# A transformer layer on one core: GpSimd's elementwise work on VectorE, quotients of the mixer's outputs on one engine, their sums of squares a block later, and one PSUM bank per head for these outputs

## The chip, the cores and the metric

One core of a Trainium2 chip. The time is microseconds of device time of one execution, as a median over runs. An engine (TensorE = PE, VectorE = DVE, ScalarE = ACT, GpSimd = POOL) takes its instructions in a fixed order; SyncE's queue (SP) issues all transfers between HBM and SBUF.

## What is computed

One layer of a hybrid backbone, for 128 context tokens and 2,048 latent tokens of width 1,024, in float32. Cut to what matters:

```python
shift1, scale1, gate1, shift2, scale2, gate2 = split(mod, 6)     # mod = silu(c) @ w_mod + b_mod
h = rmsnorm(x, norm1) * (1 + scale1) + shift1
z = h @ w_in                       # sc_b, sc_c, sc_x, q, k, v, o, gates
y_sc = sc_b * conv3(sc_c * sc_x)   # short convolution
# mLSTM, both directions, 4 heads of 128, chunks of 128 tokens:
s = (q @ k.T) * exp(dlog - m_t)
num = s @ v + w_inter * (C @ q);  den = s.sum(-1) + w_inter * (n @ q)
h_m = num / max(abs(den), exp(-m_t))
h_m = rmsnorm_per_head(h_fwd + h_bwd) * mh_norm * sigmoid(o)
x = x + gate1 * (concat(y_sc, h_m) @ w_out)
h2 = rmsnorm(x, norm2) * (1 + scale2) + shift2
a, g = split(conv3(h2 @ w_up), 2)                                # d_ff = 2816
x = x + gate2 * ((silu(g) * a) @ w_down)
y = rmsnorm(x, final_norm)
```

## The kernel before

Every large product is made of three products with operands that carry fewer bits: a float32 `a` is split into a high part `aH` (a ScalarE copy into the type that TensorE takes) and a low part `aL = a − aH` (a subtraction), and TensorE adds up `wh·hH + wh·hL + wl·hH`. So each tile of weights and of tokens costs a copy on ScalarE and a subtraction on VectorE or GpSimd before its matmuls can start. `gemm` (L192 to L199) is one block of such a product: 24 matmuls of up to 384 columns into one PSUM bank `acc`, out of a pool of four.

The program is recorded stage by stage and a scheduler then sets the order on each engine; buffers in rotation (a pool's `bufs`) decide when an instruction may start. The stages in the order of time: modulation, values and gates (vg), k, q and short convolution of the second half of the tokens (0 to some 355 us); vg of the first half; the gates' scans; **Sums** (34 units, L697 and L708: gated sums of keys and values, chunk by chunk and for a pair of heads); **Mix** (34 units, the outputs, 690 to 1020 us); the rest of the output projection and the sums of tokens for the up-projection (L229 to L236); the up-projection (L938 to L940, 44 units `j` of seven half-size products each, Strassen's scheme; weights' parts at L276, token splits at L258, drains of the banks `pa`, `pb`, `pc` at L943, L948 and L950); the down-projection (L1030 to L1032, weights' parts at L991 and L993).

Sums and Mix are short chains over several engines, so `weave` (L810) runs them as a software pipeline and puts blocks out of a list between them: q and o of the first half, its short convolution, and out_proj of four of the six token groups, 92 blocks in all, one per step in Sums, four per three steps in Mix.

A Mix unit is written in four parts, which `weave` gives to successive steps:

- load: q, k, v, the row tile `R` (512 KB, broadcast from HBM), the states.
- first: TensorE makes the scores `S` (L753); GpSimd adds the mask to the first half of `R` (L754); ScalarE takes four exponentials (L758); VectorE scales q by the second half of `R` into `qs` (L761) and multiplies the scores by the exponentials (L762).
- second: TensorE makes the outputs `y` of both heads and directions with the row sums in a 129th column (L773, L775), in a tile of two banks of which there is one; VectorE updates the state `sf` (L779), takes the divisors `den` (L783 to L785); then per head ScalarE multiplies the first direction by its reciprocal (L790), VectorE adds the second (L791), ScalarE takes the sum of squares (L793); L794 on VectorE scales it and adds EPS, GpSimd takes the power −1/2 (L795), ScalarE applies it (L797).
- third: TensorE transposes (L803), VectorE applies mh_norm and the gate o (L805), and the result is stored.

In out_proj, VectorE adds a block onto the residual (L433), ScalarE squares it (L440), and VectorE adds the squares up (L441) right behind; the statistics then sum over partitions by matmuls with ones (L122), of which those of the last group (`late`) stand ahead of the up-projection's first unit (they are called at `i == 4` of the products' loop, ahead of that product).

GpSimd's elementwise work, all of it subtractions or additions of two SBUF tiles: L108 (low parts of weights), L181 (low parts of tokens), L235 (one of the sums of tokens), L276 for three of the seven parts, L754, L993 for 704 of 1,408 columns. PSUM has eight banks: four `acc`, one `st`, one `S`, two for `y`; the jobs of mod_dve at the start (L499) write their unused product into `y` too.

## Time and profile before

| what | value |
|---|---|
| median of 3 runs | 2623.24 us (2619.05 to 2626.44) |
| the profiled execution: its span | 2622.1 us |
| TensorE busy | 2539.1 us |
| VectorE, ScalarE, GpSimd busy | 1501.3, 1066.1, 706.4 us |
| moved between HBM and SBUF | 403.25 MB, 154 GB/s |

The profiled execution is one run of its own: its time is the span, 2622.1 us from the first to the last instruction, and 1.1 us below the median. Busy time is the time in which an engine worked on an instruction; TensorE's ends are modelled. A row of waits names the waiting engine, tile and line, then what ended the wait, then the total, the number of times and the longest. A row of groups has count, busy time, mean length in ns, and the idle time ahead with its causes. The granted clock is a share of TensorE's full speed.

### The profile page before, as it was taken

Reading aid. Unit: us, or ns where it says so; the run is one execution under the profiler, and the core shown is the slowest. Engines: PE = TensorE matmul, PEld = TensorE weight load, DVE = VectorE, ACT = ScalarE, POOL = GpSimd, SP = SyncE. Lnnn points to the kernel's source line nnn. Section 1 sums busy time; section 2 is a strip of 40 time slices with the busy share of each in tenths; the row PEclk is TensorE's granted clock in tenths of the full one; section 3 lists DMA queues with packets and bytes.
Section 4 is the critical chain, followed back from the end, with each engine's and each line's share of the span. In section 5 each row is a group of like instructions: output and inputs, shape, how many; then the busy total and the mean of one; then the engine's idle time right before and its main releaser. Section 6 shows DMA issues by size and latency. Waiting matters only on the chain. (4 is left out here: it accounts for less than half of the span.)

```text
span 2622.1 us, 46918 instructions
## 1 busy us (share of the span) xinstructions
PE 2539.1 (97%) x18511; PEld 2519.2 (96%) x18511; DVE 1501.3 (57%) x2560; ACT 1066.1 (41%) x2028; POOL 706.4 (27%) x534
## 2 busy tenths in 40 slices
PE   8999999999988988899999999999999999999998
PEld 7999999999988988899999999999999999999998
DVE  3993242333457666797686669666666635353533
ACT  4521142322345454464454446554544523232411
POOL 2542242211333344221121112111111222232232
PEclk9999999999999999999999999999999999999999
DMA  8773142555467887854252224222222635454442
GB/s 280 250 254 101 57 140 85 155 180 155 152 195 242 253 256 235 267 195 139 84 178 91 79 79 165 83 83 82 83 83 90 234 113 184 156 179 150 149 139 77
DMA packets 223582, 403.25 MB, mean 154 GB/s; under 512 B 20722, under 2 KB 144770, under 8 KB 221698
## 3 DMA queue, kind: packets, MB, share of 16 engines
q1 hardware_dynamic: 223362, 400.25, 46.5%
q8 instruction: 145, 2.38, 0.4%
q14 instruction: 75, 0.61, 0.1%
HBM read 305.13 MB, written 95.04 MB: 153 GB/s over the span
## 5 line engine op out<-in xcount | busy, mean ns | idle before, releaser
L196 PE MATMUL acc<-hH,wh 128*128 128x384 f32 (+1 forms) x1536 | 516.4, 336 | 0.0
L198 PE MATMUL acc<-hH,wl 128*128 128x384 f32 (+1 forms) x1536 | 505.0, 329 | 0.0
L197 PE MATMUL acc<-hL,wh 128*128 128x384 f32 (+1 forms) x1536 | 504.7, 329 | 0.0
L938 PE MATMUL pa<-tH,wh 128*128 128x272 f32 x1408 | 410.1, 291 | 5.6 <-DVE raw L950 5.2
L940 PE MATMUL pa<-tH,wl 128*128 128x272 f32 x1408 | 409.3, 291 | 0.4 <-DVE wl L276 0.4
L1030 PE MATMUL d<-uh,wh 128*128 128x272 f32 x1408 | 406.0, 288 | 3.1 <-ACT raw L948 3.1
L939 PE MATMUL pa<-tL,wh 128*128 128x272 f32 x1408 | 407.1, 289 | 0.0
L1032 PE MATMUL d<-uh,wl 128*128 128x272 f32 x1408 | 406.9, 289 | 0.0
L1031 PE MATMUL d<-ul,wh 128*128 128x272 f32 x1408 | 404.4, 287 | 0.0
L276 POOL TENSOR_TENSOR wl<-st,wh 128x512 fp32r<-128x512 f32 x132 | 182.3, 1381 | 730.5 <-ACT wh L275 697.5
L108 POOL TENSOR_TENSOR wl<-wst,wh 128x512 fp32r<-128x512 f32 (+1 forms) x160 | 234.3, 1486 | 434.0 <-ACT wh L105 421.5
L196 PEld LDWEIGHTS acc<-hH,wh 128*128 128x128 f32 x1536 | 291.1, 190 | 1.5 <-issue 0.4
L197 PEld LDWEIGHTS acc<-hL,wh 128*128 128x128 f32 x1536 | 291.1, 189 | 1.0
L198 PEld LDWEIGHTS acc<-hH,wl 128*128 128x128 f32 x1536 | 290.5, 189 | 0.2 <-issue 0.2
L938 PEld LDWEIGHTS pa<-tH,wh 128*128 128x128 f32 x1408 | 266.8, 190 | 6.4 <-issue 5.7
L1030 PEld LDWEIGHTS d<-uh,wh 128*128 128x128 f32 x1408 | 266.9, 190 | 3.4 <-ACT raw L948 3.3
L939 PEld LDWEIGHTS pa<-tL,wh 128*128 128x128 f32 x1408 | 267.3, 190 | 0.0
L940 PEld LDWEIGHTS pa<-tH,wl 128*128 128x128 f32 x1408 | 266.6, 189 | 0.6 <-DVE wl L276 0.6
L1032 PEld LDWEIGHTS d<-uh,wl 128*128 128x128 f32 x1408 | 266.1, 189 | 0.1
L1031 PEld LDWEIGHTS d<-ul,wh 128*128 128x128 f32 x1408 | 265.3, 188 | 0.0
L993 POOL TENSOR_TENSOR wl<-st,wh 128x704 fp32r<-128x704 f32 x64 | 150.5, 2352 | 367.2 <-ACT wh L991 358.2
L884 DVE SCALAR_TENSOR_TENSOR tt<-raw,fw,tt 128x127 f32<-128x127 f32 (+4 forms) x264 | 245.7, 959 | 1.5 <-ACT tt L890 0.8
(215 smaller groups left out, 5031.6 us busy)
## 6 DMA issues: line engine op xcount, KB each, us to landing
st<-in_w_up SPq DMA_DIRECT2D x88, 512.0 KB, 4.4
st<-in_w_down SPq DMA_DIRECT2D x64, 704.0 KB, 4.2
wst<-in_w_in SPq DMA_DIRECT2D x48, 512.0 KB, 4.1
us<-uD SPq DMA_DIRECT2D x88, 272.0 KB, 4.4
R<-nD SPq DMA_DIRECT2D x34, 512.0 KB, 5.5
wm<-in_w_modr SPq DMA_DIRECT2D x32, 512.0 KB, 4.7
F<-tD SPq DMA_DIRECT2D x12, 1088.0 KB, 8.8
uD<-tt SPq DMA_DIRECT2D x22, 576.0 KB, 2.8
```

Of the source, the lines that this page charges most:

```text
L108: G.tensor_sub(wl[:, a:a + n // 2], st[:, a:a + n // 2], wh[:, a:a + n // 2].bitcast(F32))
L196: PE.matmul(acc[:, :n], w_h, hH[:, k, :n], start=(k == 0), stop=False)
L197: PE.matmul(acc[:, :n], w_h, hL[:, k, :n], start=False, stop=False)
L198: PE.matmul(acc[:, :n], w_l, hH[:, k, :n], start=False, stop=(k == KT - 1))
L276: (G if on_pool else V).tensor_sub(wl, a, wh.bitcast(F32))
L884: V.scalar_tensor_tensor(o, i, w, o, op0=ALU.mult, op1=ALU.add)
L938: PE.matmul(acc, wh[:, w], rh, start=(kk == 0 and i in (0, 1, 5)), stop=False, skip_group_check=True)
L939: PE.matmul(acc, wh[:, w], rl, start=False, stop=False, skip_group_check=True)
L940: PE.matmul(acc, wl[:, w], rh, start=False, stop=(kk == 3), skip_group_check=True)
L1030: PE.matmul(acc[b][:, :NB], wh[:, c], uh[:, q], start=(j == 0), stop=False)
L1031: PE.matmul(acc[b][:, :NB], wh[:, c], ul[:, q], start=False, stop=False)
L1032: PE.matmul(acc[b][:, :NB], wl[:, c], uh[:, q], start=False, stop=(j == FT - 1))
```

## The change

- All of GpSimd's subtractions and additions of tiles (L108, L181, L235, L276, L754, L993) go to VectorE, 434 instructions. GpSimd keeps the powers, and takes the addition of EPS (L811 after) that VectorE had (L794).
- ScalarE's step of the quotient (L790) becomes a VectorE step (L800 after); the divisors are taken per head, and stand, with the quotients, in the program ahead of the update of `sf` (L806 after). The division by 128 moves into the scale of the square.
- Each head's `y` has a bank of its own, out of three in rotation, and the Sums' products too, with two ScalarE copies for one. `acc` has three banks in rotation instead of four; in the start stage there is a pool `pj` besides, with a fourth `acc` and the two banks that mod_dve writes.
- out_proj hands its sum of squares to a list `pend`, which is emptied after the next block's output.
- The late statistics are called after the second product and may not be issued before its last matmul.
- `weave` takes a pattern: (1, 0, 1) blocks in three steps of Sums, (2, 1, 2) in Mix.

```diff
@@ weights
-            G.tensor_sub(wl[:, a:a + n // 2], st[:, a:a + n // 2], wh[:, a:a + n // 2].bitcast(F32))
+            V.tensor_sub(wl[:, a:a + n // 2], st[:, a:a + n // 2], wh[:, a:a + n // 2].bitcast(F32))
...
-            (G if on_pool else V).tensor_sub(wl, a, wh.bitcast(F32))
+            V.tensor_sub(wl, a, wh.bitcast(F32))
...
-                for e, a, b in ((G, 0, 704), (V, 704, n)):
-                    e.tensor_sub(wl[:, a:b], st[:, a:b], wh[:, a:b].bitcast(F32))
+                for a, b in ((0, 704), (704, n)):
+                    V.tensor_sub(wl[:, a:b], st[:, a:b], wh[:, a:b].bitcast(F32))
@@ accumulators
+    def accumulator():
+        pool = pa[next(turn_a) % len(pa)]
+        return pool.tile([P, 512], F32, name="acc")
...
-        pa = ph1.enter_context(tc.tile_pool(name="pa", bufs=4, space=PSUM))
+        pa = [ph1.enter_context(tc.tile_pool(name=f"pa{i}", bufs=1, space=PSUM)) for i in range(3)]
+        turn_a = count()
...
+        py = phr.enter_context(tc.tile_pool(name="py", bufs=3, space=PSUM))
@@ out_proj
                         Q.dma_start(xD[m][:, t0:t0 + n], xr[:, :n])
+                        while pend:
+                            pend.pop()()
...
-                            V.tensor_add(ss[:, :n], ss[:, :n], sq[:, :n])
+                            pend.append(lambda ss=ss[:, :n], sq=sq[:, :n]: V.tensor_add(ss, ss, sq))
@@ Mix
-                G.tensor_add(W, W, bc(maskN[:, None], [P, 2, 2, P]))
+                V.tensor_add(W, W, bc(maskN[:, None], [P, 2, 2, P]))
...
-                y = pm.tile([P, 2, 512], F32, name="y")
+                ys = [py.tile([P, 512], F32, name="y") for _ in range(2)]
...
+                for h, y in enumerate(ys):
+                    yv = y[:, :258].rearrange("p (d n) -> p d n", d=2)
+                    den = mb.tile([P, 2], F32, name="den", bufs=4)
+                    V.tensor_tensor(den, yv[:, :, 128], em[:, h], op=ALU.max)
+                    V.scalar_tensor_tensor(den, yv[:, :, 128], -1.0, den, op0=ALU.mult, op1=ALU.max)
+                    V.reciprocal(den, den)
+                    V.tensor_scalar(hv[:, h], yv[:, 0, :P], den[:, 0:1], None, op0=ALU.mult)
+                    V.scalar_tensor_tensor(hv[:, h], yv[:, 1, :P], den[:, 1:2], hv[:, h],
+                                           op0=ALU.mult, op1=ALU.add)
                 if 0 <= c < NL - 1:
...
-                    S.activation(hv[:, h], yv[:, h, 0, :P], AF.Copy, scale=den[:, h, 0:1])
...
-                V.tensor_scalar(ss, ss, 1.0 / P, EPS, op0=ALU.mult, op1=ALU.add)
+                    S.activation(sj, hv[:, h], AF.Square, scale=P ** -0.5, accum_out=ss[:, h:h + 1])
+                G.tensor_scalar(ss, ss, EPS, None, op0=ALU.add)
@@ weave
-                next(fill, None)
-                if extra and i % extra == 0:
+                for _ in range(blocks[i % 3]):
                     next(fill, None)
...
-        weave([Sums(c, hp) for c in range(NL - 1, -2, -1) for hp in range(2)], fill, 0)
-        weave([Mix(c, hp) for c in range(-1, NL) for hp in range(2)], fill, 3)
+        weave([Sums(c, hp) for c in range(NL - 1, -2, -1) for hp in range(2)], fill, (1, 0, 1))
+        weave([Mix(c, hp) for c in range(-1, NL) for hp in range(2)], fill, (2, 1, 2))
@@ products
-            if late and i == 4:
-                late.pop()()
...
+            if late and i == 1:
+                with tc.issue_after(mm.ins):
+                    late.pop()()
```

Where the instructions stand, first on TensorE, at a unit in the middle of Mix. Before (names: `S` scores, `st` the transposes of an earlier unit, `y` outputs, `acc` a projection block; in brackets the semaphores that an instruction waits for, one or more per engine or transfer queue):

```order
L198 MATMUL acc<-hH,wl 128x384
L753 MATMUL S<-q_8408,k_8404 128x128 [waits DMAHW4_49,DMAHW1_49,DVE_49]
L753 MATMUL S<-q_8408,k_8404 128x128
L803 MATMUL st<-ident,hv 128x128 [waits DVE_49,Activation_49]
L803 MATMUL st<-ident,hv 128x128 [waits Activation_49]
L773 MATMUL y<-sf_4848,qs 128x129 [waits DVE_49,PE_49]
L775 MATMUL y<-v_8321,R 128x129 [waits DMAHW2_49,DMAHW0_49]
L773 MATMUL y<-sb,qs 128x129 [waits DMAHW6_49]
L775 MATMUL y<-v_8321,R 128x129
L773 MATMUL y<-sf_4848,qs 128x129
L775 MATMUL y<-v_8321,R 128x129
```

After, at such a place (L768 is L753 of before, L820 is L803, L791 is L773, L793 is L775):

```order
L202 MATMUL acc<-hH,wl 128x384
L768 MATMUL S<-q_7995,k_7991 128x128 [waits DMAHW7_49,DMAHW1_49,DVE_49]
L768 MATMUL S<-q_7995,k_7991 128x128
L820 MATMUL st<-ident,hv 128x128 [waits DVE_49,Activation_49]
L820 MATMUL st<-ident,hv 128x128 [waits Activation_49]
L791 MATMUL y<-sf_4857,qs 128x129
L793 MATMUL y<-v_7903,R 128x129 [waits DMAHW5_49,DMAHW3_49]
L791 MATMUL y<-sb,qs 128x129 [waits DMAHW6_49]
L793 MATMUL y<-v_7903,R 128x129
L791 MATMUL y<-sf_4857,qs 128x129 [waits DVE_49,PE_49]
L793 MATMUL y<-v_7903,R 128x129
```

The first `y` matmul of a unit no longer waits on VectorE; the wait stands at the first matmul of the second head.

VectorE at such a unit, before (L433 a projection block's output, L762 the scores, L805 the output of an earlier unit, L441 a sum of squares, L779 the state, L783 to L785 the divisors, L791 the quotient):

```order
L762 TENSOR_TENSOR R<-S,R 128x2x256 [waits PE_49,Pool_49]
L805 SCALAR_TENSOR_TENSOR o_9103<-st,mhn,o_9103 128x128 [waits DMAHW3_49,PE_49]
L441 TENSOR_TENSOR ss<-ss,sq 128x384 [waits Activation_49]
L805 SCALAR_TENSOR_TENSOR o_9103<-st,mhn,o_9103 128x128
L779 SCALAR_TENSOR_TENSOR sf_4848<-sf_4848,decB,sb 128x129 [waits DMAHW2_49,PE_49]
L779 SCALAR_TENSOR_TENSOR sf_4848<-sf_4848,decB,sb 128x129 [waits PE_49]
L783 TENSOR_TENSOR den<-y,cols 128x4 [waits PE_49]
L761 TENSOR_TENSOR qs<-R,q_9346 128x512 [waits DMAHW3_49,DMAHW2_49]
L784 SCALAR_TENSOR_TENSOR den<-y,den 128x4 [waits DVE_49]
L785 RECIPROCAL den<-den 128x4 [waits DVE_49]
L791 SCALAR_TENSOR_TENSOR hv<-y,den,hv 128x128 [waits Activation_49] x2
```

After (L438 is L433 of before, L777 is L762, L822 is L805, L797 to L799 are the divisors, L806 is L779, L800 and L801 are the quotient):

```order
L438 SCALAR_TENSOR_TENSOR row<-acc,modT,row 128x384 [waits DMAHW6_49,DMAHW3_49,PE_49]
L777 TENSOR_TENSOR R<-S,R 128x2x256 [waits PE_49]
L822 SCALAR_TENSOR_TENSOR o_9575<-st,mhn,o_9575 128x128 [waits DMAHW1_49,PE_49]
L822 SCALAR_TENSOR_TENSOR o_9575<-st,mhn,o_9575 128x128
L797 TENSOR_TENSOR den<-y,cols 128x2 [waits PE_49]
L806 SCALAR_TENSOR_TENSOR sf_4857<-sf_4857,decB,sb 128x129
L798 SCALAR_TENSOR_TENSOR den<-y,den 128x2 [waits DVE_49]
L797 TENSOR_TENSOR den<-y,cols 128x2 [waits PE_49]
L799 RECIPROCAL den<-den 128x2 [waits DVE_49]
L806 SCALAR_TENSOR_TENSOR sf_4857<-sf_4857,decB,sb 128x129
L800 TENSOR_SCALAR hv<-y,den 128x128 [waits DVE_49]
L798 SCALAR_TENSOR_TENSOR den<-y,den 128x2
```

The divisors are taken head by head, the quotients wait for VectorE alone, and no sum of squares stands ahead of them.

A little later on VectorE, after (L108 a weight's low part, L769 the mask add that was L754 on GpSimd, L776 is L761 of before):

```order
L108 TENSOR_TENSOR wl<-wst,wh 128x512 [waits DMAHW0_49]
L108 TENSOR_TENSOR wl<-wst,wh 128x512
L438 SCALAR_TENSOR_TENSOR row<-acc,modT,row 128x384 [waits DMAHW7_49,PE_49]
L769 TENSOR_TENSOR R<-R,maskN 128x2x256 [waits DMAHW0_49]
L776 TENSOR_TENSOR qs<-R,q_9832 128x512 [waits DMAHW5_49]
L108 TENSOR_TENSOR wl<-wst,wh 128x512 [waits DMAHW2_49]
L438 SCALAR_TENSOR_TENSOR row<-acc,modT,row 128x384 [waits DMAHW3_49,DMAHW1_49,PE_49]
L777 TENSOR_TENSOR R<-S,R 128x2x256 [waits DVE_49,PE_49,Activation_49]
```

The mask add waits for a transfer in VectorE's order, directly ahead of the step that reads the same tile, and ahead of drains.

TensorE from the last projection block to the up-projection, before (L122 late statistics, L938 to L940 the first product):

```order
L198 MATMUL acc<-hH,wl 128x256
L122 MATMUL st<-ones,ss 128x1 [waits DVE_49,PE_49]
L122 MATMUL st<-ones,ss 128x1 x2
L938 MATMUL pa<-tH,wh 128x272 [waits DMAHW4_49,DMAHW3_49,DMAHW5_49,DMAHW1_49,DMAHW6_49,DMAHW0_49,DMAHW7_49,DVE_49,Activation_49]
L939 MATMUL pa<-tL,wh 128x272
L940 MATMUL pa<-tH,wl 128x272 [waits Pool_49]
```

After (L952 to L954 are L938 to L940):

```order
L954 MATMUL pb<-tH,wl 128x272
L122 MATMUL st<-ones,ss 128x1 x3
L952 MATMUL pa<-tH,wh 128x272 [waits DMAHW4_49,DMAHW3_49,DMAHW5_49,DMAHW2_49,DMAHW7_49,DMAHW0_49,Activation_49]
L953 MATMUL pa<-tL,wh 128x272 [waits DVE_49]
L954 MATMUL pa<-tH,wl 128x272
L122 MATMUL st<-ones,ss 128x1 [waits DVE_49]
```

The late statistics now stand behind the 48 matmuls of the first two products, and three more of the third product stand between their parts.

More of the change, by code (lines that the diff above doesn't have):

```diff
@@ L189, in make_h @@
         return apply(b, load_x(b, src, xp, "xt", 2), norm)
+    def accumulator():
+        pool = pa[next(turn_a) % len(pa)]
+        return pool.tile([P, 512], F32, name="acc")
     def gemm(w, h, n):
         (wh, wl), (hH, hL) = w, h
-        acc = pa.tile([P, 512], F32, name="acc")
+        acc = accumulator()
         for k in range(KT):
@@ L328, in vg @@
                         o = c * P - BL[b][0]
-                        acc = pa.tile([P, 512], F32, name="acc")
+                        acc = accumulator()
                         for k in range(KT):
@@ L449, in hymba_kernel @@
         hs = {}
-        with tc.tile_pool(name="start", bufs=1, side="right") as stp:
+        with tc.tile_pool(name="start", bufs=1, side="right") as stp, \
+                tc.tile_pool(name="pj", bufs=1, space=PSUM) as pj:
+            pa.append(pj)
             def mod_pe(mt):
@@ L453, in mod_pe @@
                 Q.dma_start(st, I["w_mod"][mt])
-                ps = pa.tile([P, 512], F32, name="acc")
+                ps = accumulator()
                 for k in range(KT):
@@ L705, in second @@
                 c, hp = self.c, self.hp
-                pk = pm.tile([P, 2, 512], F32, name="y")
+                pk = [py.tile([P, 512], F32, name="y") for _ in range(2)]
                 for h in range(2):
-                    PE.matmul(pk[:, h, :258], self.kT[:, h * P:(h + 1) * P],
+                    PE.matmul(pk[h][:, :258], self.kT[:, h * P:(h + 1) * P],
                               self.vw[:, h].rearrange("p d n -> p (d n)"), start=True, stop=True)
@@ L767, in second @@
                 self.o2 = load2(mb, "o2", oD, c + 1, hp)
-                y = pm.tile([P, 2, 512], F32, name="y")
-                for h in range(2):
+                ys = [py.tile([P, 512], F32, name="y") for _ in range(2)]
+                em = colsel(self.cols, EM, max(c, 0), hp)
+                hv = self.hv = mb.tile([P, 2, P], F32, name="hv", bufs=3)
+                ss = mb.tile([P, 2], F32, name="hss", bufs=2)
+                for h, y in enumerate(ys):
                     for d in range(2):
-                        o = y[:, h, d * 129:(d + 1) * 129]
+                        o = y[:, d * 129:(d + 1) * 129]
                         if c >= 0:
@@ L939, in hymba_kernel @@
                     PE.matmul(acc, wh[:, w], rl, start=False, stop=False, skip_group_check=True)
-                    PE.matmul(acc, wl[:, w], rh, start=False, stop=(kk == 3), skip_group_check=True)
+                    mm = PE.matmul(acc, wl[:, w], rh, start=False, stop=(kk == 3), skip_group_check=True)
                 if i < 3:
```

62 lines of the change are left out of this document (29 added, 33 removed).

## The prediction

> **What bounds the kernel now.** First the page: the span, then the busy time of the engines (busy us, share of the span, instructions).
>
> ```profile
> span 2622.1 us, 46918 instructions
> PE 2539.1 (97%) x18511; PEld 2519.2 (96%) x18511; DVE 1501.3 (57%) x2560; ACT 1066.1 (41%) x2028; POOL 706.4 (27%) x534
> ```
>
> TensorE is busy for 97%, and the change takes no matmul away. All that can be won is what TensorE waits (2622.1 − 2539.1 = 83 us) and what it loses to a lower granted clock. So I read its list of waits next (total us, times, longest).
>
> ```profile
> PE y L773 <- DVE hv L791: 33.3, 14, 6.9
> PE st L122 <- DVE ss L441: 8.3, 3, 6.5
> PE pa L938 <- DVE raw L950: 5.2, 3, 1.9
> PE acc L335 <- POOL hL L181: 2.2, 1, 2.2
> PE S L697 <- ACT kT L699: 0.6, 1, 0.6
> ```
>
> One row stands out: the first matmul of a mixer unit's output (L773) waits 33.3 us for the step on VectorE that empties the previous unit's `y` (L791). Where, and at what clock, the windows tell: stretch and length, busy time of PE, PEld, DVE, ACT, POOL with their counts, granted clock, DMA share, GB/s.
>
> ```profile
> 66.00:197.00 131.00, 130.47 (x888) 129.88 (x887) 124.73 (x209) 46.48 (x93) 61.70 (x47) 1.00 0.77 251
> 690.00:1020.00 330.00, 296.30 (x1890) 292.68 (x1889) 204.16 (x526) 166.26 (x499) 127.25 (x111) 0.96 0.73 229
> 850.00:858.00 8.00, 5.99 (x33) 5.78 (x32) 4.54 (x15) 3.81 (x13) 1.95 (x2) 0.79 0.77 236
> 918.00:940.00 22.00, 15.11 (x87) 14.90 (x86) 12.37 (x29) 10.37 (x28) 10.43 (x9) 0.77 0.80 247
> 1103.00:1121.00 18.00, 11.46 (x67) 11.28 (x67) 12.35 (x18) 8.50 (x14) 2.12 (x2) 0.72 0.82 295
> 1180.00:1300.00 120.00, 118.29 (x939) 118.10 (x938) 85.75 (x139) 58.67 (x104) 20.65 (x16) 1.00 0.32 107
> ```
>
> From 690 to 1020 us, where 34 mixer units are woven with projection blocks, TensorE is idle for 330 − 296.3 = 33.7 us and runs at 0.96, which costs another 330 × 0.04 = 13 us. The up-projection (1180 to 1300) is at 118.29 of 120 and full clock: nothing to win there, only to lose. Why L791 is late, three places of the timeline show (start, us, engine, line).
>
> ```profile
> 761.27 1.28 ACT L758 ACTIVATE R<-R,cols 128x128 f32<-128x128 f32 x4 [5.19 <-POOL R L754]
> 762.84 0.35 DVE L791 SCALAR_TENSOR_TENSOR hv<-y,den,hv 128x128 f32<-128x128 f32 x1 [2.44 <-ACT hv L790]
> 819.74 2.88 DVE L407 TENSOR_TENSOR hL<-xt,hH 128x384 fp32r<-128x384 f32 x2
> 926.21 1.31 DVE L441 TENSOR_TENSOR ss<-ss,sq 128x384 f32<-128x384 f32 x1 [1.96 <-ACT sq L440]
> 932.82 0.77 PE L773 MATMUL y<-sf,qs 128*128 128x129 f32 x2 [6.89 <-DVE hv L791]
> ```
>
> The quotient's ScalarE half (L790) stands behind exponentials that wait for GpSimd's mask add; VectorE's subtractions of two SBUF inputs take 1.44 us each here, while GpSimd works; and the squares' sum (L441) holds VectorE's queue for ScalarE. The change touches all three, and gives the next unit another bank besides.
>
> **The change part by part.** Mixer stage. The groups of 690 to 1020 us (count, busy us, mean ns, idle before):
>
> ```profile
> L108 POOL TENSOR_TENSOR wl<-wst,wh 128x512 fp32r<-128x512 f32 x44 | 60.2, 1389 | 73.8 <-ACT wh L105 67.5 <-DMA R<-nD 3.7 <-PE y L775 2.6
> L754 POOL TENSOR_TENSOR R<-R,maskN 128x512 f32<-128x512 f32 x31 | 42.2, 1360 | 102.1 <-DMA R<-nD 100.1 <-PE st L803 1.9
> L779 DVE SCALAR_TENSOR_TENSOR sf<-sf,decB,sb 128x129 f32<-128x129 f32 x60 | 29.6, 527 | 0.3 <-PE y L773 0.3
> L761 DVE TENSOR_TENSOR qs<-R,q 128x512 f32<-128x512 f32 x31 | 24.2, 781 | 4.7 <-DMA R<-nD 4.6
> L791 DVE SCALAR_TENSOR_TENSOR hv<-y,den,hv 128x128 f32<-128x128 f32 x68 | 23.8, 350 | 45.7 <-ACT hv L790 45.4
> L762 DVE TENSOR_TENSOR R<-S,R 128x512 f32<-128x512 f32 x33 | 22.5, 682 | 2.7 <-PE st L803 2.7
> L441 DVE TENSOR_TENSOR ss<-ss,sq 128x384 f32<-128x384 f32 x22 | 16.2, 735 | 27.0 <-ACT sq L440 27.0
> L794 DVE TENSOR_SCALAR hss<-hss 128x2 f32<-128x2 f32 x34 | 10.1, 296 | 13.5 <-ACT sj L793 12.6 <-POOL wl L108 0.5
> L785 DVE RECIPROCAL den<-den 128x4 f32<-128x4 f32 x34 | 6.0, 176 | 0.9
> ```
>
> VectorE has 204 us of work there. It gets 44 L108 and 31 mask adds at the 0.69 of a 512-wide step (L762): 52 us; 68 quotients at L791's 0.35: 24; the three `den` steps per head instead of per unit, 34 × 3 × 0.17 (L785 is the longest): 17. It loses L794's 10. And GpSimd no longer stretches its steps: L779 by 60 × 0.18, L441 by 22 × 0.18, L761 by 31 × 0.1, others a little, some 22 us. That makes 265 us. TensorE without waits and at full clock needs 330 − 33 − 13 = 284. So VectorE fits by 19 us if each step costs its full length; it costs less:
>
> ```profile
> 756.65 0.35 DVE L779 SCALAR_TENSOR_TENSOR sf<-sf,decB,sb 128x129 f32<-128x129 f32 x1
> 756.91 0.61 DVE L384 SCALAR_TENSOR_TENSOR yr<-cr,scw,yr 128x378 f32<-128x378 f32 x1
> ```
>
> A step of 0.35 us is followed 0.26 later: 0.09 less each, over some 700 steps (526 and what is added) about 60 us. VectorE's work then takes 205 of 284 us. The three banks for `y` let the next unit's first head start with no wait, and its second only needs the first head of the unit before, so the drain has a projection block more than now. I take the 33 us of L773 as gone. What is late next: the stage's transfers. They have a share of 0.73 over 330 us; in 284 that is 0.85, and no window above goes over 0.82. At 0.82 the stage takes 330 × 0.73 / 0.82 = 294 us. I take 294, a gain of **36** (bounds: 284 to 330). Twelve blocks come over from the Sums stage with their own matmuls, VectorE steps and loads, and count on neither side.
>
> Three small things cost nothing: GpSimd's sum with EPS in place of L794 lengthens the chain to the next transpose by less than the block that lies between; three accumulator banks for four still leave two whole blocks for a drain; the Sums' second ScalarE copy goes into an engine at 166 of 330.
>
> On the clock, the window 850 to 858 lost 8 × 0.21 = 1.7 us behind this wait:
>
> ```profile
> 852.40 0.46 PE L773 MATMUL y<-sf,qs 128*128 128x129 f32 x2 [2.01 <-DVE hv L791]
> ```
>
> So short waits that remain may cost clock too. [...]
>
> Late statistics. The wait of 6.5 us (L122 for L441) is followed by slow matmuls:
>
> ```profile
> 1112.74 1.41 PE L122 MATMUL st<-ones,ss 128*128 128x1 f32 x6 [6.54 <-DVE ss L441]
> 1114.61 0.43 PE L940 MATMUL pa<-tH,wl 128*128 128x272 f32 x1
> 1114.84 0.43 PE L938 MATMUL pa<-tH,wh 128*128 128x272 f32 x1
> ```
>
> They start 0.23 us apart; 939 of them in the 120 us from 1180 are 0.13 apart. The first 24 run so: 2.4 us. With 48 up matmuls put ahead, 48 × 0.13 = 6 us cover the sum. Gain **9** (0 to 9). The deferred sums (`pend`) are the same instructions a block later; what they bring is in the stage above.
>
> Sums stage. Of 34 units 11 now follow another with no block between. The only wait there today is 0.6 (L697 for L699); 11 of them are 6.6. I take +**3** (0 to 10).
>
> Start. VectorE is at 124.73 of 131 us already from 66 to 197:
>
> ```profile
> L499 DVE SCALAR_TENSOR_TENSOR y<-wm,cB 128x1024 f32<-128x1024 f32 x64 | 89.9, 1405 | 3.3 <-DMA wm<-in_w_modr 2.4
> ```
>
> GpSimd's 61.7 us there come over at half their length (0.69 for 1.39), some 30 at most, and without GpSimd L499 gets shorter (L779 by a third; a tenth to a third of 89.9 is 9 to 30). The modulation that L499 computes is not needed before the output projection, so a late finish costs nothing; L181's 2.2 on TensorE goes: −**1** (−3 to +2). Where the first half's values and gates begin, the weights' subtractions now stand behind a step that waits for the tokens: +**1.5** (−1 to +4, by waits of 1 to 2 us in the list).
>
> Up-projection. Three subtractions of 0.69 per unit and half, 2.1 us of 21 us, go to VectorE. VectorE's waits ahead of the drains L950, and rows of the weights' subtractions:
>
> ```profile
> DVE raw L950 <- PE pc L940: 77.2, 72, 1.1
> DVE raw L950 <- PE pa L940: 74.4, 73, 1.1
> DVE raw L950 <- PE pb L940: 73.2, 69, 1.6
> DVE wl L993 <- ACT wh L991: 136.8, 59, 7.4
> L276 POOL TENSOR_TENSOR wl<-st,wh 128x512 fp32r<-128x512 f32 x132 | 182.3, 1381 | 730.5 <-ACT wh L275 697.5
> ```
>
> 225 us of idle time stand ahead of drains, and 132 × 0.69 = 91 us come in; VectorE goes from 85.75 of 120 to some 97. About 1 us a gap takes one 0.69: it fits. At the units where the tokens' splits run too it will not always: +**4** (−5, L938's wait gone, to +12, 0.3 a unit). Down: 64 × 0.93 = 60 us go into 137 idle: 0.
>
> Sum against the span: −36 − 9 + 3 − 1 + 1.5 + 4 = −37.5, so 2622.1 − 37.5 = 2584.6. The median of the runs, 2623.2, is 1.1 above the span: **2586 us**.
>
> **The rivals.** (A) VectorE becomes the mixer stage's bound. If each step costs its full length, 265 us, plus the waits in its queue that stay (L761's 4.7, L762's 2.7, and some 30 behind TensorE and ScalarE), it needs about 302; TensorE then waits some 18 us, and with as much clock as now, 13, the stage is 315: 2586 + 21 = 2607. For it: 265 of 284. Against it: the rows 0.26 apart. [...] Chance 0.13.
>
> (B) Slower: GpSimd's wait for the transfer of `R` (100.1 us in this stage, behind nothing that matters) moves into VectorE's queue, ahead of the drains. VectorE has 19 to 79 us free to take it up, so 22 to 80 us reach TensorE. The middle, 51, with the clock that waits cost in this stage (13 beside 33), is 71: a stage of 284 + 71 = 355 in place of 294, so 2647. Against: L761 reads the same tile and VectorE waited only 4.6 us there. It decides if the mask add reaches the queue's head over 1.5 us before `R` lands in most units. Chance 0.12.
>
> (C) Drains late in the up-projection: one 0.69 a unit on TensorE, 44 × 0.69 = 30 instead of 4: 2612. For it: VectorE at 81%. Against: gaps of 1 us in the rows. Chance 0.07.
>
> (D) The change frees `y` and no time: TensorE waits for `S`, `R` or weights instead, the stage stays at 330: 2622. For it: transfers at 0.73 to 0.8. Against: in the list no transfer keeps L773 or L775. Chance 0.09.
>
> **How the numbers follow.** The forecast keeps 0.59. A measurement here tells 0.3% (8 us) from no change. Faster: 0.59 + 0.13 + 0.05 of C = 0.77; same: 0.02 of C and D, 0.11; slower: B, 0.12. The range goes from 2562 (the stage at 284, up at −5, Sums at 0, rounded) up to 2622, which takes in A, C and D's middle.
>
> **What would show it.** Right: the `y` matmul (L791 after) waits under 10 us in all; DVE's share rises to some 64% (1501 + 91 + 60 + 110 + 34 × 0.69 + the quotients, less the contention); L779's mean falls to 0.35; the late L122 waits for nothing. A shows in DVE over 95% busy in the mixer stage; B in DVE's waits for `R` above 40 us; C in L950's row among TensorE's waits; D in TensorE's waits for DMA. I am wrong if the mixer stage keeps over 20 us of waits.

## The result, and the profile after

The kernel after takes 2576.8 us (median of 4 runs, 2571.7 to 2578.6) against 2624.7 before in the same runs: a ratio of 0.9824, with a 95% interval of 0.9808 to 0.9841. My 2586 was 9 us too high; the direction and the rough size were right. The profiled execution spans 2574.4 us, 47.7 less than that of before.

The page of after, span and busy times:

```profile
span 2574.4 us, 46544 instructions
PE 2525.0 (98%) x18511; PEld 2506.9 (97%) x18511; DVE 1621.1 (63%) x3130; ACT 1054.1 (41%) x1994; POOL 64.3 (2%) x134
```

GpSimd's busy time fell by 642 us, and VectorE's rose by only 120. TensorE's busy time falls by 14 us though its instructions are the same, and its mean granted clock rises from 0.988 to 0.992.

Of TensorE's list of waits, after, the rows of the mixer stage and of the first up matmul. The 33.3 us for the outputs' bank have become 0.2; what is left there are single waits.

```profile
PE st L122 <- DVE o L822: 5.9, 1, 5.9
PE S L768 <- DVE R L777: 4.0, 2, 2.9
PE pa L952 <- DVE row L438: 3.4, 1, 3.4
PE y L791 <- DVE den L799: 0.2, 1, 0.2
```

To see where the time went, I cut each trace at the same events (the first gate transposes, the first scores of Mix, its last transpose, the first up and the first down matmul). The windows of before (length, busy PE, PEld, DVE, ACT, POOL, clock, DMA share, GB/s):

```profile
436.80:688.30 251.50, 250.17 (x1416) 242.04 (x1415) 82.24 (x182) 69.72 (x158) 46.85 (x33) 0.99 0.50 153
688.30:1019.30 331.00, 297.30 (x1897) 293.68 (x1896) 204.66 (x526) 166.26 (x499) 126.55 (x111) 0.96 0.73 228
1019.30:1114.00 94.70, 85.36 (x549) 84.16 (x548) 67.30 (x121) 40.67 (x81) 31.84 (x26) 0.96 0.80 260
1114.00:2066.10 952.10, 941.44 (x7421) 939.54 (x7421) 692.89 (x992) 494.19 (x846) 194.72 (x143) 0.99 0.32 111
```

And of after:

```profile
437.00:638.80 201.80, 201.79 (x1151) 192.74 (x1149) 73.16 (x192) 66.63 (x181) 0.00 (x0) 1.00 0.58 179
638.80:990.90 352.10, 341.98 (x2184) 340.82 (x2184) 248.36 (x762) 154.06 (x444) 38.38 (x70) 0.98 0.73 222
990.90:1074.00 83.10, 77.84 (x519) 77.27 (x517) 64.40 (x141) 38.99 (x79) 1.95 (x2) 1.00 0.88 286
1074.00:2016.30 942.30, 939.08 (x7427) 937.59 (x7427) 760.00 (x1133) 497.57 (x846) 1.92 (x2) 1.00 0.32 112
```

The stages are gates and Sums, Mix, the rest up to the first up matmul, and the up-projection. Blocks of the projections moved between the first three. The count of one of a block's three kinds of matmul, eight to a block, tells how many; in Sums, before and after:

```profile
L196 PE MATMUL acc<-hH,wh 128*128 128x384 f32 x392 | 139.8, 357 | 0.0
L200 PE MATMUL acc<-hH,wh 128*128 128x384 f32 x304 | 107.9, 355 | 0.0
```

That is 49 blocks and 38. Mix has 48 and 60, the rest one less: Mix takes over eleven from Sums and one from the rest. So these three are compared together: 677.2 us before, 637.0 after, 40.2 less. The up-projection lost 9.8. The start (436.8 and 437.0) and the down-projection (556.0 and 558.1) stayed. Mix itself no longer has its 33.7 us of idle TensorE but 10.1.

### The profile page after: what moved, and what is told of

It is laid out like the page before. It is cut to its first block, busy times and chain, and to the rows that moved or that the text cites. A ratio compares the mean times of both kernels' runs of the same rounds, so it can differ in the third digit from the quotient of the medians.

```text
span 2574.4 us, 46544 instructions
## 1 busy us (share of the span) xinstructions
PE 2525.0 (98%) x18511; PEld 2506.9 (97%) x18511; DVE 1621.1 (63%) x3130; ACT 1054.1 (41%) x1994; POOL 64.3 (2%) x134
## 4 chain that ended last, share of the span: by engine, by line
PE 87%; DMA 6%; DVE 4%; issue 1%; ACT 1%; POOL 0%; SPq 0%; DVEq 0%; ACTq 0%; POOLq 0%
PE acc L200 8%; PE acc L202 8%; PE acc L201 8%; PE d L1049 7%; PE pa L952 7%; PE d L1047 7%; PE pa L954 7%; PE d L1048 7%; PE pa L953 6%; PE pb L954 3%; PE pb L952 3%; PE pb L953 3%; PE pc L954 2%; PE pc L952 2%; PE pc L953 2%; PE y L721 1%
## 5 line engine op out<-in xcount | busy, mean ns | idle before, releaser
L952 PE MATMUL pa<-tH,wh 128*128 128x272 f32 x1408 | 409.0, 291 | 3.8 <-DVE row L438 3.4
L954 PE MATMUL pa<-tH,wl 128*128 128x272 f32 x1408 | 407.8, 290 | 0.1
L952 PEld LDWEIGHTS pa<-tH,wh 128*128 128x128 f32 x1408 | 265.6, 189 | 4.5 <-DVE row L438 3.6
L954 PEld LDWEIGHTS pa<-tH,wl 128*128 128x128 f32 x1408 | 265.3, 189 | 0.3 <-DVE wl L280 0.3
L1008 ACT ACTIVATE wh<-st 128x1408 fp32r<-128x1408 f32 x64 | 88.3, 1380 | 356.2 <-PE d L1048 196.2
L954 PE MATMUL pb<-tH,wl 128*128 128x272 f32 x704 | 203.8, 290 | 0.8 <-DVE wl L280 0.8
L1010 DVE TENSOR_TENSOR wl<-st,wh 128x704 fp32r<-128x704 f32 x128 | 108.3, 887 | 152.5 <-ACT wh L1008 152.4
```

What stands on the lines that cost most here:

```text
L952: PE.matmul(acc, wh[:, w], rh, start=(kk == 0 and i in (0, 1, 5)), stop=False, skip_group_check=True)
L954: mm = PE.matmul(acc, wl[:, w], rh, start=False, stop=(kk == 3), skip_group_check=True)
L1008: S.activation(wh, st, AF.Copy)
L1010: V.tensor_sub(wl[:, a:b], st[:, a:b], wh[:, a:b].bitcast(F32))
```

## The experiments

Each ratio is to the kernel before, run on the same chip, with its 95% interval; the kernel after has 0.9824 (0.9808 to 0.9841). The chips differ a little (before took 2618.4 to 2624.7 us on them), so kernels are compared by their ratios. "Mix" is the length between the same two events as above, 352.1 us after, and can be compared among kernels with the new pattern of blocks. "Sums to up" is gates, Sums, Mix and the rest together: 637.0 after, 677.2 before. "Up" is the up-projection's length: 942.3 after, 952.1 before. Each length is read from one trace. The two kernels whose edit lies behind Mix have 352.6 and 356.2 there, and where nothing of the up-projection is changed its length goes from 939.2 to 942.3; Sums to up goes from 634.5 to 643.0 where GpSimd has the work of after. Differences within these spreads are not told from nothing.

| kernel | ratio | interval | Mix | Sums to up | Up |
|---|---|---|---|---|---|
| all six groups back on GpSimd | 0.9986 | 0.9976 to 0.9995 | 371.5 | 671.3 | 954.2 |
| before, with the move alone | 0.9883 | 0.9868 to 0.9897 | other pattern | 655.8 | 941.7 |
| one `y` tile | 0.9842 | 0.9828 to 0.9857 | 359.6 | 643.0 | 940.4 |
| mask add on GpSimd | 0.9844 | 0.9828 to 0.9860 | 358.0 | 640.3 | 942.0 |
| idle work on GpSimd | 0.9960 | 0.9948 to 0.9972 | 356.5 | 650.0 | 951.7 |
| up-projection's parts on GpSimd | 0.9863 | 0.9838 to 0.9889 | 352.6 | 635.6 | 951.7 |
| late statistics at the old place | 0.9834 | 0.9811 to 0.9857 | 356.2 | 640.8 | 942.3 |
| quotient's half on ScalarE | 0.9830 | 0.9804 to 0.9856 | 351.5 | 634.5 | 939.5 |
| weights' L108 on GpSimd | 0.9859 | 0.9841 to 0.9876 | 356.4 | 650.9 | 939.2 |
| L108 and the mask add on GpSimd | 0.9924 | 0.9910 to 0.9938 | 374.2 | 671.2 | 939.4 |
| sums of squares at once | 0.9828 | 0.9812 to 0.9844 | 356.1 | 639.3 | 939.8 |
| quotient's half on ScalarE, statistics in another bank | 0.9805 | 0.9783 to 0.9828 | 353.4 | 637.6 | 942.3 |

**Everything but the move.**

```diff
-            V.tensor_sub(wl[:, a:a + n // 2], st[:, a:a + n // 2], wh[:, a:a + n // 2].bitcast(F32))
+            G.tensor_sub(wl[:, a:a + n // 2], st[:, a:a + n // 2], wh[:, a:a + n // 2].bitcast(F32))
...
```

and so at the other five places.

> The kernel after, with all six groups of subtractions and additions back on GpSimd (434 instructions); banks, quotients, deferred sums, late statistics and weave as after. Theory 1 (the bank per head carries the mixer's gain: with it a drain that is a few us late keeps nobody): the mixer stage stays within 5 us of after, only the up-projection gives back some 8 us (its waits for L950 and for low parts of weights), so about 2585 us. Theory 2 (the move carries it: GpSimd stretched VectorE's steps of two SBUF inputs to twice their length, and that made the drains late): TensorE's waits in the mixer stage come back to 20 us or more, and the time is 2600 us or above. What is seen either way: the mean of the state's update goes back from 0.34 to about 0.5 us.

2616.8 us: nearly all of the gain is gone. Theory 2 came: TensorE is idle for 23.8 us of Mix again (371.50 − 347.67), and the state's update (L806) takes 543 ns, 339 after. What TensorE waits for isn't what I had in mind. Its two longest rows for `S` and `y`, then ScalarE's and VectorE's:

```profile
PE S L768 <- DVE R L777: 9.2, 4, 4.0
PE y L791 <- DVE den L799: 4.6, 5, 1.6
```

```profile
ACT R L773 <- POOL R L769: 63.6, 29, 6.9
```

```profile
DVE ss L448 <- ACT sq L447: 52.3, 23, 6.1
```

ScalarE stands for 63.6 us behind the mask add on GpSimd, and VectorE for 52.3 behind ScalarE's squares (8.8 in all after). The outputs' banks keep the wait for `y` short; the lateness comes out at the scores' bank instead, and at a lower clock (0.97 in Mix, 0.98 after).

**The move alone, on the kernel before.**

```diff
-                G.tensor_add(W, W, bc(maskN[:, None], [P, 2, 2, P]))
+                V.tensor_add(W, W, bc(maskN[:, None], [P, 2, 2, P]))
...
```

> The kernel before, with the six groups on VectorE and nothing else changed: one y tile, the quotient's half on ScalarE, sums of squares at once. Theory 1 (bank): the mixer stage stays as slow as before (TensorE waits for L791 about 30 us), the up-projection gains its 8, about 2613 us. Theory 2 (move): waits for L791 fall under 15 us and the time to about 2595 us. A third outcome, the move alone harms: the mask add's wait for R in VectorE's queue makes L791 later still, waits over 40 us, 2630 us or more; then it is the banks that make the move bearable.

2588.4 us: 1.17% of the whole 1.76%. The time is what theory 2 gave, its number of waits is not: `y` still costs

```profile
PE y L773 <- DVE hv L791: 24.2, 12, 4.8
```

Move alone 1.17%, all else alone 0.14%, both together 1.76%: each needs the other for the last 0.45%. In the up-projection the move alone brings all of the gain (941.7 us). From Sums to up it brings 21.4 of the 40.2 us; the rest comes only with the other parts on top of it. The late statistics, at their old place here, wait 1.7 us instead of 6.5.

**One tile for `y`.**

```diff
-                ys = [py.tile([P, 512], F32, name="y") for _ in range(2)]
+                ys = py.tile([P, 2, 512], F32, name="y")
+                ys = [ys[:, h] for h in range(2)]
```

> The kernel after, with one tile of two banks for the outputs y of both heads (and for the Sums' products), as before; all else as after. Theory 1 (bank): the first y matmul of a unit waits for the whole drain again, 20 us or more of waits in the mixer stage, about 2600 us. Theory 2 (move): the drain is short enough now (VectorE alone, some 3 us, against a block of 4.2 us), waits under 8 us, about 2583 us.

```profile
PE y L793 <- DVE hv L803: 16.5, 8, 4.3
```

The wait is back at half its size, as theory 1 said, Mix is 7.5 us longer, and yet the total is within the error of after (0.9842 and 0.9824, intervals overlap): with the drain on time the bank is worth a few us at most.

**The mask add alone on GpSimd.**

```diff
-                V.tensor_add(W, W, bc(maskN[:, None], [P, 2, 2, P]))
+                G.tensor_add(W, W, bc(maskN[:, None], [P, 2, 2, P]))
```

> The kernel after, with the mask add alone (34 instructions) back on GpSimd. Theory A (the 46.8 us that VectorE waits for R at the mask add still cost TensorE something: the waits of 2.9 us for the scores' bank at 880 and of 5.9 at 917 stand behind such waits): waits of TensorE in the mixer stage fall from 10 to under 4 us and the stage by 8 to 12 us with the clock, 2567 us. Theory B (VectorE had that time free; TensorE's two waits are from elsewhere): the same as after within 3 us, 2577 us.

Theory B, by the time. In after, VectorE waits for `R` at the mask add (the group of 640 to 980 us; last columns: idle before, and why):

```profile
L769 DVE TENSOR_TENSOR R<-R,maskN 128x512 f32<-128x512 f32 x31 | 21.4, 689 | 46.9 <-DMA R<-nD 46.8
```

Taking that wait off VectorE's queue gains nothing: 2577.3 us, Mix 358.0, and TensorE's wait for the scores' bank is 10.9 us instead of 4.0. That fits VectorE having had the time free. It isn't a clean test of it, since the mask add also takes twice as long on GpSimd (a mean of 1360 ns in Mix before, 689 on VectorE after), and the exponentials start later for it.

**Idle work on GpSimd.**

```diff
             V.tensor_sub(wl[:, a:a + n // 2], st[:, a:a + n // 2], wh[:, a:a + n // 2].bitcast(F32))
+            G.tensor_sub(idle[:, :512], wh[:, a:a + 512].bitcast(F32), wh[:, a:a + 512].bitcast(F32))
...
```

> The kernel after, and besides GpSimd gets an idle subtraction for nearly every one that was taken from it (160 of L108, 132 of the up-projection's, 128 of 352 columns for the 64 of the down-projection): same engine, same kind with two SBUF inputs, started by the same ScalarE copy, written to a scratch tile that nobody reads. Nobody waits for GpSimd's result. Theory 1 (contention: GpSimd's work beside VectorE stretches VectorE's steps, and that is what the move took away): the time goes back most of the way, 2600 to 2617 us, VectorE's squares and state updates are longer again, and the up-projection's loss is back at 15 us or more. Theory 2 (latency: the low parts and the mask came late, because GpSimd takes 1.4 us where VectorE takes 0.7): the same as after, 2577 us within 4.

2608.6 us, as theory 1 had it: the kernel loses 1.36%, though nobody waits for the work's result. This is not a share of the change's 1.76%: VectorE has all of the moved work here, as after, and GpSimd works beside it, as before. Where, the windows say (start, Mix, up-projection of this kernel):

```profile
0.00:449.70 449.70, 424.57 (x2916) 422.34 (x2917) 283.23 (x514) 145.07 (x271) 109.71 (x116) 0.98 0.51 165
656.90:1013.40 356.50, 340.71 (x2184) 338.22 (x2183) 271.18 (x760) 152.95 (x442) 102.27 (x120) 0.99 0.72 218
1099.70:2051.40 951.70, 941.12 (x7426) 937.96 (x7426) 780.37 (x1132) 494.30 (x846) 202.26 (x137) 1.00 0.32 111
```

The start is 12.7 us longer, Sums to up 13.0 (Mix 4.4 of it), the up-projection 9.4. The start's loss is no part of what the change gained: with the useful work on GpSimd the start is no longer than after (436.0 us with all six groups back, 437.0 after). Nor is it contention alone: there ScalarE's next copy waits for the idle work to let go of its input buffer, a row of the whole trace that stands in the start entirely:

```profile
ACT wh L106 <- POOL idle L110: 11.0, 6, 2.5
```

Behind the start there is no such wait. With the same instructions VectorE is busy for 780 us instead of 760 in the up-projection: its steps are stretched. How far a step can stretch, the squares' sums of the down-projection show, in before, after and this kernel:

```profile
L1046 DVE TENSOR_TENSOR ss<-ss,sq 128x544 f32<-128x544 f32 x27 | 55.7, 2062 | 0.0
```

```profile
L1063 DVE TENSOR_TENSOR ss<-ss,sq 128x544 f32<-128x544 f32 x27 | 19.4, 718 | 0.7 <-ACT sq L1062 0.7
```

```profile
L1069 DVE TENSOR_TENSOR ss<-ss,sq 128x544 f32<-128x544 f32 x27 | 33.7, 1248 | 0.7 <-ACT sq L1068 0.7
```

2062 ns beside GpSimd's 704-wide steps, 718 alone, 1248 beside idle ones of half the size. One such pair in before:

```profile
2560.51 2.41 POOL L993 TENSOR_TENSOR wl<-st,wh 128x704 fp32r<-128x704 f32 x1 [5.79 <-ACT wh L991]
2561.28 2.23 DVE L1046 TENSOR_TENSOR ss<-ss,sq 128x544 f32<-128x544 f32 x1
```

GpSimd's step ends at 2562.92, VectorE's sum 0.59 us later. The drains with one input in PSUM keep their length, before and after:

```profile
L950 DVE TENSOR_TENSOR raw<-pa,c 128x272 f32<-128x272 f32 x88 | 38.5, 439 | 74.4 <-PE pa L940 74.4
L964 DVE TENSOR_TENSOR raw<-pa,c 128x272 f32<-128x272 f32 x88 | 38.6, 440 | 45.0 <-PE pa L954 44.9
```

Why the sums stretch and the drains don't, no run shows. The stretched sums cost the down-projection no time that can be told: VectorE is busy for 232.87 of its 556.0 us before, and it takes 558.1 after and 557.3 with idle work. So contention, as theory 1 has it, is shown as a cost for the up-projection and for Sums to up, where it is 13.0 of the 34.3 us that all six groups cost there.

**The up-projection's parts on GpSimd.**

```diff
-        yield part(a11)
+        yield part(a11, True)
...
```

> The kernel after, with the three subtractions per unit of the up-projection alone (132) on GpSimd, as before. My prediction charged their move with +4 us; in the traces the up-projection lost 17.8 us over its pitch before and 7.3 after. If the move is the gain there, this kernel loses about 10 us against after (2587 us), all of it in the up-projection. If the gain came with the late statistics' new place or with chance, the same as after within 3 us.

The first: 951.7 us for the up-projection against 942.3, all else as after, 2580.6 us in all. It is the same 951.7 that idle work gave. That alone doesn't prove that the low parts' later arrival costs nothing, as VectorE has 65 us less to do in this window than after (694.9 us) and idle work leaves it all there. But TensorE waits for GpSimd's parts just once:

```profile
PE pc L954 <- POOL wl L280: 0.9, 1, 0.9
```

TensorE is idle for 11.2 us of this stage, 3.2 after, in many waits of at most 3 us. So what counts is when VectorE's steps end and not how much it has to do; which of its steps make the 8 us wasn't worked out.

**Late statistics at the old place.**

```diff
+            if late and i == 4:
+                late.pop()()
...
-            if late and i == 1:
-                with tc.issue_after(mm.ins):
-                    late.pop()()
```

> The kernel after, with the late statistics at their old place, ahead of the first unit's fifth product in the program and so right behind the last projection block on TensorE. My prediction gave their new place 9 us (a wait of 6.5 and 2.4 of slow clock). Theory 1 (the place): 2586 us, with a wait of L122 of 5 us or more. Theory 2 (the sum of squares was late because VectorE was; with the move it is on time, as the move alone showed a wait of 1.7 us at most): within 3 us of after, 2578 us.

```profile
1076.48 1.01 PE L122 MATMUL st<-ones,ss 128*128 128x1 f32 x6 [3.75 <-DVE ss L448]
```

Theory 2 by the time, but not by its reason: a wait of 3.75 us is there, and yet no time is lost (2573.3 us): in after, the first up matmul waits 3.4 us at the same spot for the output of the last block (L952 for L438, above). The new place swapped one wait for another.

**Quotient's half on ScalarE.**

```diff
-                    V.tensor_scalar(hv[:, h], yv[:, 0, :P], den[:, 0:1], None, op0=ALU.mult)
+                    S.activation(hv[:, h], yv[:, 0, :P], AF.Copy, scale=den[:, 0:1])
```

> The kernel after, with the first half of the quotient on ScalarE again (68 steps), all else as after. Theory 1 (the quotient on one engine is needed, since ScalarE's step stands behind exponentials and weights' copies): waits for y's bank come back, some 10 us, 2587 us. Theory 2 (with three banks and the mask add on time the hop over ScalarE fits): 2577 us within 4.

Theory 2: 2572.0 us, Mix 351.5. That part of the change does nothing that can be told.

**Blocking on GpSimd's queue.** Mix lost 19.4 us with all six groups back, 4.4 with idle work, 5.9 with the mask add. Two runs to find what the rest is. The first puts L108 alone on GpSimd (the first diff above, nothing else).

> The kernel after, with the low parts of the start's and the mixer's weights alone (160 instructions) on GpSimd. With all six groups on GpSimd the mixer stage lost 37.9 us over its pitch against 18.6 after; with idle work of the same kind beside it 23.0; with the mask add alone 24.4. Theory B (blocking: GpSimd's queue held the mask add behind weights and weights behind the mask add's transfer, ScalarE's exponentials behind that, and the squares behind them): one of the two alone does little, the mixer stage loses 20 to 25 us, and the time is 2577 to 2584 us. Theory L (a weight's low part that takes 1.4 us instead of 0.7, and stretches VectorE, is enough): 33 us or more in the mixer stage, 2592 us.

The second puts L108 and the mask add there.

> The kernel after, with those weights' low parts and the mask add on GpSimd (194 instructions), the up- and down-projection's on VectorE. Theory B (blocking between the two on one queue): 33 to 38 us lost in the mixer stage, as with all six groups there, and 2592 us or above, with VectorE waiting over 30 us for the squares at the sums of squares (8.8 after, 47.5 with all six). Theory L: as with the weights alone. If neither comes, some other of the six groups must act on this stage, and the cause stays open.

Both times are where theory B put them. L108 alone: Mix 356.4 (+4.3), 2583.6 us. Both: Mix 374.2 (+22.1), 2600.6 us, more than twice the two singles together (4.3 + 5.9 = 10.2). From Sums to up, L108 alone costs 13.9 us, about as much as idle work (13.0), the mask add alone 3.3, both 34.2, and all six groups 34.3. So half of this stage's loss, some 17 us, appears only when the two are together. Waits of ScalarE and VectorE with both:

```profile
ACT R L773 <- POOL R L769: 76.9, 30, 7.4
```

```profile
DVE ss L448 <- ACT sq L447: 55.6, 25, 6.1
```

Theory B's reason is not shown by them, since the mask add alone on GpSimd has nearly the same two rows and loses 3.3 us:

```profile
ACT R L773 <- POOL R L769: 62.1, 28, 5.4
DVE ss L448 <- ACT sq L447: 34.5, 16, 6.3
```

Nor does GpSimd hold the mask add behind weights: with both, 20 of its 34 mask adds wait for the transfer of `R` (74.4 us). The other direction is there, weights right behind a mask add that waited, and the power's steps behind these:

```profile
719.04 1.77 POOL L769 TENSOR_TENSOR R<-R,maskN 128x512 f32<-128x512 f32 x1 [6.08 <-DMA R<-nD]
720.77 2.54 POOL L108 TENSOR_TENSOR wl<-wst,wh 128x512 fp32r<-128x512 f32 x2
723.40 0.22 POOL L811 TENSOR_SCALAR hss<-hss 128x2 f32<-128x2 f32 x1
```

A second account fits as well: a late mask costs little while VectorE can catch up, and it can't when its steps are stretched (the squares' sums L448 have a mean of 549 ns after, 552 with the mask add, 722 with L108, 801 with both). No run separates the two, so the cause of these 17 us stays open.

In before, TensorE's waits for `y` have both beginnings. The exponentials at 761.27 that the prediction shows, 5.19 us behind the mask add, stand ahead of a wait of 3.55 us. The longest wait, the 6.89 us at 932.82, has another beginning (TensorE's row of the first, then ScalarE, VectorE and GpSimd ahead of the second, whose sum at 926.21 the prediction shows):

```profile
764.41 0.47 PE L773 MATMUL y<-sf,qs 128*128 128x129 f32 x2 [3.55 <-DVE hv L791]
924.71 1.06 ACT L105 ACTIVATE wh<-wst 128x1024 fp32r<-128x1024 f32 x1 [2.20 <-DMA wst<-in_w_out]
925.67 0.51 ACT L440 ACTIVATE sq<-row 128x384 f32<-128x384 f32 x1
927.45 1.34 DVE L779 SCALAR_TENSOR_TENSOR sf<-sf,decB,sb 128x129 f32<-128x129 f32 x1
928.79 1.68 DVE L761 TENSOR_TENSOR qs<-R,q 128x512 f32<-128x512 f32 x1
925.84 5.74 POOL L108 TENSOR_TENSOR wl<-wst,wh 128x512 fp32r<-128x512 f32 x4 [5.36 <-ACT wh L105]
```

The square stands behind a weight's copy that waited for a transfer, not for GpSimd. Then three steps of VectorE take 1.31, 1.34 and 1.68 us beside GpSimd's weights, where steps of the same lines had taken 0.56, 0.35 and 0.67 (at 921.66, 923.91 and 913.41): 2.75 us of stretch in a wait of 6.89.

**Sums of squares at once.**

```diff
-                            pend.append(lambda ss=ss[:, :n], sq=sq[:, :n]: V.tensor_add(ss, ss, sq))
+                            V.tensor_add(ss[:, :n], ss[:, :n], sq[:, :n])
```

> The kernel after, with each sum of squares written right behind its square again, not a block later. With the move alone the mixer stage still lost 37.7 us over its pitch, after it 18.6; one y tile gave back 7, ScalarE's quotient nothing. Theory 1 (the deferred sums are the rest): about 10 us in the mixer stage and 2586 us, with VectorE's wait for squares at 20 us or more in it. Theory 2 (each of these parts covers for the other, and the new pattern of blocks does the rest): within 4 us of after.

Theory 2: 2575.4 us, VectorE's wait for squares is 16.3 us over the whole kernel instead of 8.8, and the ratio doesn't tell it from after.

**A faster version?** ScalarE's quotient as above, and:

```diff
-                    stats(grp, sss)
+                    stats(grp, sss, accumulator)
```

> A try for a faster version: the kernel after, with the quotient's first half on ScalarE again, and with the statistics of the output projection in a bank out of the accumulators' rotation, not in the one bank of the transposes, for which TensorE waits 5.9 us in the middle of the mixer stage (row L122 for L822). If that bank is what the wait is for, the row goes and the time is 4 to 8 us under after, 2570 us; if the matmul merely stands there while VectorE is late with the sum itself, the wait stays under another name, within 3 us of the kernel with ScalarE's quotient alone (2572).

The wait of 5.9 us (L122 for L822) is gone, 0.5 is left; Mix has 353.4 us, as others wait longer. 2569.9 us, 0.9805 with an interval of 0.9783 to 0.9828: it may be a little faster than after (0.9808 to 0.9841), but that isn't shown.

## Why the prediction came out

**Mixer stage, with Sums and the late wait: 36 + 6.5 − 3 = 39.5 forecast, 40.2 measured.** The sum came out by luck, as two of its terms were off by 7 us in opposite directions. By the windows, and at 24 × 0.174 = 4.18 us a block (the spacing of its matmuls: 917.28, 917.45, 917.63 in before), Mix without its twelve added blocks takes 302.0 us, 29.0 less than before, where I had 36. Sums with eleven blocks less would take 205.6 and took 201.8, a gain of 3.8 where I had a loss of 3. The rest, with one block less, gained 7.4.

The explanation was only partly right too: I named the three banks, the quotient and the deferred sums beside the move. One at a time each of these parts can be taken out of after for 0.0 to 0.2%, while taking out the move costs 1.6%. Yet the move alone brings only 21.4 of the 40.2 us, so some of the other parts, or the new pattern, do matter together. Of the signs that I named, `y`'s wait is 0.2 us, VectorE's share 63%, the state's update 339 ns, and the late L122 waits for nothing.

**Late statistics, −9.** The wait of 6.5 us went, but not because of the new place: with the move alone it is 1.7 us at the old one, and in after another wait of 3.4 stands there.

**Up-projection, +4 forecast, −9.8 measured: the step that failed.** Some 2.4 of it are the slow matmuls that I booked with the late statistics. I counted how much work VectorE gets (91 us) and where it fits, and let the contention that I had counted in Mix out of the sum here. VectorE's busy time rose by 67 us in this stage (692.89 to 760.00), not by 91, and the drains' row among TensorE's waits (L938 for L950, 5.2 us) went. What the contention is worth was measured twice: 20 us of VectorE's time with idle work (780.37 for 760.00), and 9.4 us of the stage, with idle work as with these parts on GpSimd.

**Start, down-projection.** +0.5 forecast and +0.2 measured for the start: VectorE, full there, took the work over without loss (it is busy for 123.65 of the 131 us from 66 to 197, 124.73 before). The down-projection's 0 was +2.1.

**What is left over in Mix.** I took 10 us over the 284, as transfers would come to a share of 0.82. It is 18 (302.0): TensorE is idle for 10.1 us, of which the two rows above make 9.9 (5.9 for the one bank of the transposes, 4.0 for the scores' bank), and the clock of 0.98 costs 352 × 0.02 = 7. The transfers' share stayed at 0.73, so the 10 had the wrong cause.

**Rivals.** (A), VectorE as the bound, didn't come: it is busy for 248 of 352 us, 71%. That this is close to my 205 of 284, 72%, is luck. A window's busy time counts overlapping steps once: from 690 to 1020 in before, the groups' times add up to 227 us and the window says 204. So I took the overlap of the 526 steps off twice; only the 211 added ones (44 + 31 + 68 + 102 − 34) had 0.09 us each to give, which makes 246 of 284, so this rival was nearer than I took it to be. The steps' spacing shows in two rows of after:

```profile
915.79 0.35 DVE L800 TENSOR_SCALAR hv<-y,den 128x128 f32<-128x128 f32 x1
916.05 0.15 DVE L798 SCALAR_TENSOR_TENSOR den<-y,den 128x2 f32<-128x2 f32 x1
```

0.26 us from one start to the next, for a step of 0.35, as before. (B): its mechanism came, its price did not. VectorE's wait for `R` is 46.8 us, over the 40 that I had named as the sign, and the kernel with the mask add on GpSimd, without that wait, is no faster. A wait on an engine with room is no sign by itself; I should have named the next engine's wait. (C) and (D) didn't come.

**The clock.** It was low behind a short wait here too. After the wait for the scores' bank, and in the window around it:

```profile
883.79 1.22 PE L768 MATMUL S<-q,k 128*128 128x128 f32 x4 [2.93 <-DVE R L777]
```

```profile
878.00:892.00 14.00, 11.07 (x55) 10.75 (x54) 10.87 (x31) 4.92 (x16) 1.45 (x2) 0.76 0.87 276
```

At a mean of 0.76 over 14 us, up to 14 × 0.24 us are lost beside the 2.9 of waiting. The clock was 1.00 from 870 to 878 us, 0.50 from the end of the wait to 886, and 1.00 again from 890 to 900.

**What stays open.** Taken out one at a time, the parts besides the move add up to 0.4% (0.18, 0.04, 0.06, 0.10), none of them clear of the error, and all of them on top of the move bring 0.6%. The new pattern of blocks wasn't taken out alone; it, or the parts covering for one another, is the rest. That weights and mask add on GpSimd cost 17 us more together than apart was measured; whether by the order of GpSimd's queue or because stretched steps leave VectorE no room to catch up was not.

## What to carry to other kernels

Don't judge a side engine by its busy share: GpSimd was busy for 27%, TensorE waited 4.1 us in all for its low parts (L108, L181, L276), and yet moving its work alone gained 1.2%, in part because it had made VectorE's steps longer (the sums of squares at L1046 took 2062 ns beside it, 718 in after). Idle work of the same kind, whose result nobody reads, is a way to measure that; look where it loses time that the useful work did not, as it did in the start here. Count what leaves as well as what comes: GpSimd's 642 us cost VectorE 120 more, since VectorE does such a step in half the time (a mean of 690 ns for the up-projection's 512 columns, 1381 on GpSimd) and its other steps got shorter (the state's update 339 ns, 527 before). And where an engine's wait grows, ask which engine waits for it before calling it a cost.

## What the runs showed of the hardware

A subtraction of 128 × 512 took 1.38 to 1.5 us on GpSimd (L276, L108 in before) and 0.68 on VectorE (L108 after). Idle GpSimd work of the same kind stretched VectorE's sums of two 128 × 544 SBUF tiles from 718 to 1248 ns, and the up-projection by 9.4 us, as much as useful work there did. The drains with an input in PSUM (L950, 439 ns before and 440 after) weren't stretched. Around a wait of TensorE of 2.9 us the mean granted clock was 0.76 over 14 us.
